# Handing x, conditioning and spatial matrices over transposed, fused dot products for conditioning, and a front on two column blocks of v

## The chip, the core and the metric

The program runs on one core of one Trainium2 chip. The metric is the device time of one execution in microseconds. The kernel before took 2926.15, 2928.23 and 2930.01 us in three runs (median 2928.23). What the host does to lay out the inputs before the launch is not part of the time. TensorE is written PE, VectorE DVE, ScalarE ACT, GpSimd POOL; SP is the engine on which nearly all transfers are issued.

## The reference, cut to what matters

```python
def gmlp_layer(x, c, ada_w, ada_b, norm_g, w_in, sgu_g, w_s, b_s, w_out):    # layer A
    shift, scale, gate = ada_mod(c, ada_w, ada_b, 3)      # split(silu(c) @ ada_w + ada_b)
    h = rms_norm(x, norm_g) * (1 + scale) + shift
    u, v, z = jnp.split(h @ w_in, 3, axis=-1)             # 1024 -> 3 x 2048
    u = jax.nn.gelu(u)
    v = rms_norm(jax.nn.gelu(v), sgu_g)
    w_causal = jnp.tril(w_s)                              # 8 groups of 128x128
    mixed = jnp.einsum('gts,bcsge->bctge', w_causal, v) + b_s...
    y = u * mixed * jax.nn.silu(z)
    return x + gate * (y @ w_out)
...
def shared_kv(...):        # its own shift, scale from kv_ada_w; h @ w_kv gives keys and values
def dilated_layer(...):    # layer B: its own shift, scale, gate; q and z from b_w_in,
                           # attention over three dilations, x + gate * (o * silu(z) @ w_out)
```

x is 2048 x 1024 float32. The conditioning vector c is one row of 1024; it goes through silu and three matrices (1024 x 3072, 1024 x 2048, 1024 x 3072) to give the shifts, scales and gates.

## The kernel before, in words

The 2048 tokens are worked in four quarters Q of 512. For each quarter layer A makes v (2048 columns), u, z and the output, and then layer B makes keys, values, q and its z; the attention of one quarter runs as side work beside layer A of the next. h stands transposed in SBUF: 1024 features as 8 tiles k of 128 rows, 512 tokens along a row. A float32 product is made of three rounded matmuls: h is split into a high part (hAh) and a low part (hAl), each weight tile into high and low too, and `mm3` issues high x high, low x high, high x low. The high part of a weight is a copy on ACT, the low part a subtraction on DVE (`split`).

For Q = 0 the dense product of v is written plainly: `dense` handles 512 columns j, loops over 2 pairs of token tiles, 8 tiles k and 2 token tiles. For Q = 1 to 3 v is made by `dense_s2` for two blocks of 1024 columns at a time, from 7 half-size products each: 14 products of 24 matmuls of 128x512. The operands of some of them are sums of quarters of h: s1, s2, s3 and s4. They come about so: `make_hA` makes h for the next quarter and stores it in DRAM (tile hd); `sums_A` loads it back as four pieces (m<-hd); DVE adds and subtracts them (s1, s3, s2, s4 in this order); each is split into high and low (sA). The order of the first six products of v is: block 4 with h's quarter 11, block 4 with 22, block 4 with 12, block 5 with 11, block 4 with s2, block 5 with 12. The gelu of the first product's columns is evacuated behind the third.

**Front.** `begin` serves Q = 0 and the first 512 columns of v. It loads x by token rows, squares on ACT, scales rows by 1/rms on DVE and transposes with PE into hf. Conditioning there: `add` accumulates 8 row tiles of the matrix times silu(c) into a 128x512 tile (DVE, scalar-tensor-tensor), one column group c of four at a time; `affine` sums that tile over its partitions by matmuls against a column of ones (pc_a). The product over these 512 columns is a plain float32 matmul (pd_v<-wf,hf, two hardware matmuls each), the other three blocks go through `dense`.

**Side work** stands in a list of generators; `tick` is called as PE's products go into the program and advances the generators by `rate` steps per unit; `drain` runs what is left. A z block is three `dense_s` blocks of 8 ticks' worth beside which `make_hA` of the next quarter advances at rate 0.9. Then comes `drain`, then v of the next quarter. The conditioning of shared keys and of layer B and the gate of layer A (`ada_acc`, `column_sums`, `ada_gate`) run as side work in Q = 0, the gate of layer B in Q = 3.

A scheduler with a cost model decides each engine's order when the program is built; the order is fixed from then on and each engine takes its queue strictly in it. Buffers come from pools: 6 large tiles (16 KB per partition), 8 weight tiles (w), 6 raw weight tiles (raw), 4 input tiles (xin), 6 evacuation tiles.

Of the kernel before, what the change touches and what calls it, by code (L numbers as in the profile page):

```python
# [15 lines left out]
ALU = mybir.AluOpType  # L16
# [18 lines left out]
def trunk(ctx, tc, out, x, c, a_ada_w, a_ada_b, a_norm_g, a_w_in, a_sgu_g, a_w_spatial,  # L35
          a_b_spatial, a_w_out, kv_ada_w, kv_ada_b, kv_norm_g, w_kv, k_norm_g, b_ada_w,
          b_ada_b, b_norm_g, b_w_in, b_q_norm_g, b_w_out, dbg=None):
# [27 lines left out]
    gd = dp.tile([2, D], F32, name="gd")  # L65
    wod = dp.tile([2, KT, P, 2, 512], F32, name="wod")
# [39 lines left out]
    ones = cp.tile([P, 1], F32, name="ones")  # L106
    nc.vector.memset(ones, 1.0)
# [3 lines left out]
    def columns(rows, nm):  # L111

        vec = evt(f"vec{nm}")
        nc.vector.memset(vec[:, 0:P], 0.0)
        off, o = [], 0
        for r in rows:
            n = r.shape[0] // P
            nc.sync.dma_start(vec[o:o + n, 0:P], r.rearrange("(k p) -> k p", p=P))
            off.append(o)
            o += n  # L120
        pv = pst(f"pv{nm}")
        nc.tensor.transpose(pv[:, 0:P], vec[:, 0:P], ident)
        t = cp.tile([P, o], F32, name=f"cols{nm}")
        nc.vector.tensor_copy(t, pv[:, 0:o])
        return [t[:, i:i + r.shape[0] // P] for i, r in zip(off, rows)]

    def load_x(t):
        xt = xp.tile([P, D], F32, tag="xin", name=f"x_{t}")
        nc.sync.dma_start(xt, x[t * P:(t + 1) * P, :])
        return xt  # L130

    xts = [load_x(0)]
    c_c, ang_c, aab_c = columns([c[0], a_norm_g[0], a_ada_b[0, 0:2 * D]], "a")
    sc = cp.tile([P, KT], F32, name="sc")
    xts += [load_x(1)]
    late = {}

    def late_constants():
        kg, bg, kb, bb, sgu, kn, qn = columns(
            [kv_norm_g, b_norm_g[0], kv_ada_b, b_ada_b[0, 0:2 * D], a_sgu_g[0], k_norm_g,  # L140
             b_q_norm_g[0]], "b")
        late.update(kg=kg, bg=bg, kb=kb, bb=bb, sgu=sgu)
        gqk = cp.tile([P, 1], F32, name="gqk")
        nc.vector.tensor_scalar(gqk, kn, qn, float(P) ** -0.5, ALU.mult, ALU.mult)
# [24 lines left out]
    def ada_acc(res, w, c0, nm):  # L169

        acc = evt(f"acc_{nm}")
        for k in range(KT):
            if k % 2 == 0:
                wt = xp.tile([P, 2, 512], F32, tag="xin", name=f"aw_{nm}{k}")
                nc.sync.dma_start(wt, w[k * P:(k + 2) * P, c0:c0 + 512].rearrange("(k p) n -> p k n", p=P))
            if k == 0:
                nc.vector.tensor_scalar(acc, wt[:, 0, :], sc[:, 0:1], None, ALU.mult)
            else:
                nc.vector.scalar_tensor_tensor(acc, wt[:, k % 2, :], sc[:, k:k + 1], acc, ALU.mult, ALU.add)
            if k % 2:  # L180
                yield
        res.append(acc)

    def column_sums(acc, nm):

        pc = pst(f"pc_{nm}")
        for j in range(4):
            nc.tensor.matmul(pc[:, j:j + 1], acc[:, j * P:(j + 1) * P], ones, start=True, stop=True)
        return pc[:, 0:4]

    later = []

    def delayed(gen):

        for _ in gen:
            for job in later:
                job[0] -= 1
            while later and later[0][0] <= 0:
                later.pop(0)[1]()
            yield  # L200
        while later:
            yield
            later.pop(0)[1]()
# [648 lines left out]
    def begin(aff):  # L852
# [31 lines left out]
        def transposes(c, prs=(0, 1)):  # L884
            if c not in pcs:
                pcs[c] = []
# [826 lines left out]
```

## Time and profile before

| what | value |
|---|---|
| three runs | 2926.15, 2928.23, 2930.01 us |
| profiled execution, span | 2930.7 us; the page gives no other time of it |
| granted TensorE clock, mean | 0.998 |
| first plain matmul of v | 18.53 us |
| first, second block of v done | about 53.3, 78.2 us |
| v of Q = 1, 2, 3 begins | 638.29, 1268.21, 1909.66 us |
| x loads from row layout | 16 of 512 KB, median 4.5 us from issue to landing |
| hd stores | 24 of 256 KB, median 5.0 us |
| loads of hd | 12 of 512 KB, median 6.4 us |

How to read the rows: in the timeline, a row is start, duration, engine, line of the kernel, operation, what it writes <- what it reads, form, count of neighbours put together, and in brackets the idle time of the engine before it with what ended it. In the table of groups, the fields behind the bar are total us, mean ns, and idle time before. SPq is SP's queue of transfers. Durations of neighbouring instructions overlap somewhat, so the pitch from start to start is the price in a stream.

### The profile page before, as it was taken

To read this page: it belongs to the slowest core of one execution; us is meant where nothing else is said; L and a number is where in the kernel's file an instruction comes from. 1 tells how busy PE (TensorE), PEld (TensorE's weight loads), DVE (VectorE), ACT (ScalarE), POOL (GpSimd) and SP (SyncE) were. 2 spreads that over 40 slices of the span, in tenths; PEclk is the share of its full clock that TensorE was granted. 3 is DMA by queue.
4 is the path that set the end of the run, shared out by engine and by line. 5 is a ranking of instruction groups with operands and counts; after the bars stand their busy time and mean duration, and the time that the engine had idled before them with its cause. 6 is when DMAs were issued, how large, how long until landed. Compare 5 with 4: busy or idle time off the path is not lost.

```text
span 2930.7 us, 45684 instructions
## 1 busy us (share of the span) xinstructions
PE 2890.4 (99%) x14642; PEld 2422.7 (83%) x14642; DVE 2166.7 (74%) x4038; ACT 1639.0 (56%) x3378; POOL 758.4 (26%) x1043
## 2 busy tenths in 40 slices
PE   8999999999999999999999999999999999999999
PEld 5788888888888878888888888888888888888887
DVE  6878666787777886877677776877769776888682
ACT  4323355767676365676555365674646366876441
POOL 1057522330000513501223213501414221122312
PEclk9999999999999999999999999999999999999999
DMA  8899976796889976887435976875337967789653
GB/s 285 272 311 336 308 244 184 257 306 203 282 294 315 334 241 210 265 289 249 158 120 202 344 226 203 296 262 162 105 109 260 322 202 224 256 271 332 216 172 112
DMA packets 393813, 713.54 MB, mean 243 GB/s; under 512 B 41723, under 2 KB 141277, under 8 KB 393573
## 3 DMA queue, kind: packets, MB, share of 16 engines
q1 hardware_dynamic: 393572, 710.63, 72.6%
q8 instruction: 116, 1.90, 0.3%
q14 instruction: 125, 1.02, 0.1%
HBM read 552.53 MB, written 157.95 MB: 242 GB/s over the span
## 4 chain that ended last, share of the span: by engine, by line
PE 40%; DMA 3%; issue 3%; DVE 3%; POOL 1%; ACT 1%; SPq 0%; POOLq 0%; ACTq 0%; DVEq 0%
PE po L1453 3%; PE pd_kv L280 3%; PE pd_z L324 2%; PE pd_z L322 2%; PE pd_z L323 2%; PE pd_o3a L280 1%; PE pd_u L322 1%; PE pd_u L324 1%; PE pd_u L323 1%; PE pd_o2a L280 1%; PE pd_v3b L280 1%; PE pf L1637 1%; PE pf L1638 1%; PE pf L1639 1%; DMA qt<-qd 1%
## 5 line engine op out<-in xcount | busy, mean ns | idle before, releaser
L280 PE MATMUL pd_kv<-w_kv,hkh 128*128 128x512 f32 x672 | 209.5, 393 | 1.4 <-DVE w_kv L252 1.3
L322 PE MATMUL pd_u<-hAh,w_u 128*128 128x512 f32 x512 | 207.5, 405 | 0.0
L322 PE MATMUL pd_z<-hAh,w_z 128*128 128x512 f32 x512 | 204.1, 399 | 0.0
L324 PE MATMUL pd_u<-hAh,w_u 128*128 128x512 f32 x512 | 201.0, 393 | 2.3 <-DVE w_u L252 2.3
L323 PE MATMUL pd_u<-hAl,w_u 128*128 128x512 f32 x512 | 200.2, 391 | 0.0
L324 PE MATMUL pd_z<-hAh,w_z 128*128 128x512 f32 x512 | 200.2, 391 | 0.0
L323 PE MATMUL pd_z<-hAl,w_z 128*128 128x512 f32 x512 | 199.5, 390 | 0.0
L1453 PEld LDWEIGHTS po<-kv,pT 128*128 128x128 f32 x1200 | 147.9, 192 | 13.0 <-ACT pT L1299 3.7
L251 ACT ACTIVATE w_u<-raw_u 128x512 fp32r<-128x512 f32 x128 | 79.2, 630 | 135.4 <-DMA raw_u<-in_a_w_in_dram 56.7
L1453 PE MATMUL po<-kv,pT 128*128 128x128 f32 x1200 | 151.2, 276 | 3.6 <-ACT pT L1299 2.5
L251 ACT ACTIVATE w_z<-raw_z 128x512 fp32r<-128x512 f32 x128 | 79.6, 628 | 133.9 <-PE pd_z L324 60.6
L280 PEld LDWEIGHTS pd_kv<-w_kv,hkh 128*128 128x128 f32 x672 | 125.9, 189 | 28.6 <-DVE w_kv L252 2.6
L1401 POOL TENSOR_TENSOR dg<-pr,ident 128x256 f32<-128x256 f32 x38 | 30.9, 813 | 437.2 <-DVE stat L1448 226.6
L252 DVE TENSOR_TENSOR w_z<-raw_z,w_z 128x512 fp32r<-128x512 f32 x128 | 109.4, 868 | 44.9 <-ACT w_z L251 44.6
L280 PE MATMUL pd_kv<-w_kv,hkl 128*128 128x512 f32 x336 | 131.2, 391 | 0.0
L1393 ACT ACTIVATE pr<-pr,stat,rt 128x256 f32<-128x256 f32 (+1 forms) x192 | 104.2, 544 | 33.2 <-DVE stat L1387 20.0
L1226 POOL TENSOR_SCALAR s_q<-s_q 128x4 f32<-128x4 f32 x96 | 26.6, 277 | 351.3 <-DVE s_q L1225 238.8
L252 DVE TENSOR_TENSOR w_u<-raw_u,w_u 128x512 fp32r<-128x512 f32 x128 | 94.1, 745 | 30.8 <-ACT w_u L251 30.0
L324 PEld LDWEIGHTS pd_u<-hAh,w_u 128*128 128x128 f32 x512 | 96.4, 188 | 24.2 <-DVE w_u L252 3.1
L251 ACT ACTIVATE w_q<-raw_q 128x512 fp32r<-128x512 f32 x144 | 88.8, 627 | 48.3 <-PE pd_kv L280 11.2
L252 DVE TENSOR_TENSOR w_q<-raw_q,w_q 128x512 fp32r<-128x512 f32 x144 | 95.8, 687 | 24.9 <-ACT w_q L251 22.9
L324 PEld LDWEIGHTS pd_z<-hAh,w_z 128*128 128x128 f32 x512 | 96.1, 188 | 20.7
(904 smaller groups left out, 8553.1 us busy)
## 6 DMA issues: line engine op xcount, KB each, us to landing
raw_q<-in_b_w_in_dram SPq DMA_DIRECT2D x144, 256.0 KB, 3.4
w_o<-wtd SPq DMA_DIRECT2D x72, 512.0 KB, 5.2
raw_u<-in_a_w_in_dram SPq DMA_DIRECT2D x128, 256.0 KB, 4.2
raw_z<-in_a_w_in_dram SPq DMA_DIRECT2D x128, 256.0 KB, 3.6
wtd<-cs SPq DMA_DIRECT2D x56, 512.0 KB, 4.1
qt<-qd SPq DMA_DIRECT2D x96, 260.0 KB, 3.6
raw_v<-in_a_w_in_dram SPq DMA_DIRECT2D x96, 256.0 KB, 4.1
od<-ot SPq DMA_DIRECT2D x96, 256.0 KB, 3.0
```

What stands on the lines that cost most here:

```text
L251: nc.scalar.activation(hi, src, AF.Copy)
L252: nc.vector.tensor_tensor(lo, src, hi.bitcast(F32), ALU.subtract)
L280: last_mm[0] = nc.tensor.matmul(pt, a, u[:, w, :], start=f, stop=e, skip_group_check=more)
L322: nc.tensor.matmul(pts[i], wh, hh[:, k, :], start=k == 0, stop=False)
L323: nc.tensor.matmul(pts[i], wh, hl[:, k, :], start=False, stop=False)
L324: nc.tensor.matmul(pts[i], wl, hh[:, k, :], start=False, stop=k == KT - 1)
L1393: nc.scalar.activation(pr[:, i, :], pr[:, i, :], AF.Exp, bias=mneg[:, i:i + 1], scale=u["rt"][:, h:h + 1], accum_out=lsum[:, i:i + 1])
L1401: nc.gpsimd.tensor_tensor(dg, prev, ident.unsqueeze(1).broadcast_to([P, hp, P]), ALU.mult)
L1453: nc.tensor.matmul(po[:, h * P:(h + 1) * P], u["pT"][h // hp][:, h % hp, j, :], u["kv"][:, j, kh, 1, :], start=j == 0, stop=j == nk - 1)
L1637: nc.tensor.matmul(pt, yb[:, 0, k, :], w_[:, 0, :], start=k == 0, stop=False)
L1638: nc.tensor.matmul(pt, yb[:, 0, k, :], w_[:, 1, :], start=False, stop=False)
L1639: nc.tensor.matmul(pt, yb[:, 1, k, :], w_[:, 0, :], start=False, stop=k == KT - 1)
```

## The change

The host now hands over, laid out differently: x as before and also transposed (xt: quarter, feature, k, token); the three conditioning matrices transposed and cut into tiles of 128 outputs x 1024 (a_ada, kv_ada, b_ada); the spatial matrices transposed (spatial); the vectors of norms and biases packed as columns of one 128 x 106 array (cols). The computation is the same.

- Conditioning: 128 outputs stand on the partitions and their 1024 weights along the row; `ada_dot` multiplies by silu(c), broadcast to all partitions (scb), sums along the row and adds the bias, in one DVE instruction and a second that reads the accumulator. The sums over partitions on PE are gone. The gate of layer B moves from Q = 3 to Q = 0. Gates go to DRAM (gd) as columns.
- `make_hA` loads x by rows for the squares and xt for the values; 1/rms goes through DRAM (rd) to be broadcast as a row (rb). Values are multiplied by rb (DVE), then scale and shift (ACT), high part (ACT), store to hd, low part (POOL), k by k for all 512 tokens. There are no PE transposes. It yields 27 times where it yielded 20, at the same rate.
- `begin` sums squares with PE against ones, makes the broadcast of 1/rms with PE, and then for k = 0 to 7 does both column blocks 0 and 1 by three rounded matmuls, with the conditioning of k + 1 made beside. `dense` then makes blocks 2 and 3.
- The spatial matrices are one load.

```diff
+    def ada_dot(dst, w, b):
+        nc.vector.tensor_tensor_reduce(out=w, in0=w, in1=scb, scale=1.0, scalar=b, op0=ALU.mult,
+                                       op1=ALU.add, accum_out=dst)
+    def ada_col(dst, w, j0, bo, nm):
+        for j in range(KT):
+            t = xp.tile([P, D], F32, tag="xin", name=f"aw_{nm}{j}")
+            nc.sync.dma_start(t, w[j0 + j])
+            ada_dot(dst[:, j:j + 1], t, bo[:, j:j + 1])
+            yield
...
+    def ada_gate(w, bo, i, nm):
+        col = sp.tile([P, 16], F32, tag="rt", name=f"gc_{nm}")
+        yield from ada_col(col, w, 2 * KT, bo, nm)
+        nc.sync.dma_start(gd[i:i + 1, :].rearrange("o (k p) -> p (o k)", p=P), col[:, 0:KT])
...
     def make_hA(res, Q, aff):
...
+        zs = [xp.tile([P, 2, QT], F32, tag="xin", name=f"xT{Q}_{k2}") for k2 in range(0, KT, 2)]
+        for i, z in enumerate(zs):
+            nc.sync.dma_start(z, xt[Q, :, 2 * i:2 * i + 2, :])
+        yield
+        nc.sync.dma_start(rd[Q].rearrange("t p -> p t"), r[:, 0:TPQ])
         yield
         yield
-        for t in range(TPQ):
-            nc.scalar.activation(xts[t], xts[t], AF.Copy, scale=r[:, t:t + 1])
-            yield
-        for pr in range(2):
-            for k2 in range(0, KT, 2):
-                norm_T(xts[2 * pr:2 * pr + 2], pr, [hA + aff], f"a{Q}_{pr}_", (k2,))
-                yield
+        rb = bcast(rd[Q:Q + 1].rearrange("o t p -> o (t p)"), f"rb{Q}")
+        yield
+        yield
+        for k in range(KT):
+            z = zs[k // 2][:, k % 2, :]
+            nc.vector.tensor_tensor(z, z, rb, ALU.mult)
+            yield
+            h = evt(f"h_a{Q}_{k}")
+            nc.scalar.activation(h, z, AF.Identity, scale=aff[0][:, k:k + 1], bias=aff[1][:, k:k + 1])
+            nc.scalar.activation(hA[0][:, k, :], h, AF.Copy)
+            nc.sync.dma_start(hd[:, :, k, :].rearrange("r p t -> p r t"),
+                              h.rearrange("p (r t) -> p r t", r=2))
+            nc.gpsimd.tensor_tensor(hA[1][:, k, :], h, hA[0][:, k, :].bitcast(F32), ALU.subtract)
+            yield
...
     def begin(aff):
...
+        for k in range(KT):
+            h = xT[:, k, :]
+            if k == 1:
+                nc.vector.tensor_tensor(h, h, rb, ALU.mult)
+            if k:
+                nc.scalar.activation(h, h, AF.Identity, scale=aff[0][:, k:k + 1], bias=aff[1][:, k:k + 1])
+                split(hA[0][:, k, :], hA[1][:, k, :], h)
+            if k + 1 < KT:
+                units(k + 1)
+                affine(k + 1)
+            if k + 2 < KT:
+                load(k + 2)
+                nc.gpsimd.tensor_tensor(xT[:, k + 2, :], xT[:, k + 2, :], rb, ALU.mult)
+            for j in range(2):
+                for t in range(TPQ):
+                    sl = slice(t * P, (t + 1) * P)
+                    mm3(pts[j][t], hA[0][:, k, sl], hA[1][:, k, sl], us[k][j], k == 0, k == KT - 1)
```

**Where the order moves: DVE in the front.** aw is a piece of the conditioning matrix, acc_a its accumulation, affa scale and shift, pc_a the sums from PE, colsa the vectors, r_a 1/rms. Before, from the first accumulation on:

```order
L878 TENSOR_SCALAR acc_a_273<-aw_207,sc 128x512
L879 SCALAR_TENSOR_TENSOR acc_a_273<-aw_207,sc,acc_a_273 128x512 x7
L902 TENSOR_TENSOR affa_194<-pc_a_318,colsa 128x2
L903 TENSOR_TENSOR affa_193<-pc_a_318,colsa 128x2
L904 SCALAR_TENSOR_TENSOR affa_193<-affa_193,colsa 128x2
L878 TENSOR_SCALAR acc_a_343<-aw_222,sc 128x512
L941 TENSOR_SCALAR x_216<-x_216,r_a_315 128x1024
L879 SCALAR_TENSOR_TENSOR acc_a_343<-aw_222,sc,acc_a_343 128x512
```

Now, from the third dot product (k = 1) on, the rows up to the weights of k = 2; L152 ISA is the dot and, with one column, the reading of its accumulator, L188 the low parts of weights w_v and of h (hAl):

```order
L152 ISA aw_315,affa_181<-aw_315,scb,vecs 128x1024
L152 ISA affa_181 128x1
L188 TENSOR_TENSOR w_v_1_0_365<-raw_v_1_0_366,w_v_1_0_365 128x512
L188 TENSOR_TENSOR w_v_1_0_370<-raw_v_1_0_371,w_v_1_0_370 128x512
L829 SCALAR_TENSOR_TENSOR affa_180<-affa_180,vecs 128x1
L152 ISA aw_378,affa_180<-aw_378,scb,vecs 128x1024
L152 ISA affa_180 128x1
L829 SCALAR_TENSOR_TENSOR affa_180<-affa_180,vecs 128x1
L152 ISA aw_378,affa_181<-aw_378,scb,vecs 128x1024
L152 ISA affa_181 128x1
L188 TENSOR_TENSOR hAl_187<-xT_188,hAh_186 128x512
L188 TENSOR_TENSOR w_v_2_0_410<-raw_v_2_0_411,w_v_2_0_410 128x512
```

The chain of eight accumulations and the wait for PE's sums are gone; two dots for each k stand among the subtractions.

**SP at the boundary, ahead of v of Q = 1.** hd is h in DRAM, m1 the loads of its four pieces, raw_v the weights of v (raw_v1511 those of the fourth product), zd the stores of z. Before:

```order
L259 DMA raw_v14t4_0_6037<-wt4_3_125 128x512
L708 DMA hd_104<-h_a1_1_6_0_5892 128x512
L259 DMA raw_v14t4_1_6042<-wt4_3_125 128x512
L1240 DMA zd_101<-zb00_2_5914 128x512
L1240 DMA zd_101<-zb00_3_5917 128x512
L828 DMA m1_1_5976<-hd_104 128x1024
L259 DMA raw_v14t4_2_6047<-wt4_3_125 128x512
L259 DMA raw_v14t4_3_6052<-wt4_3_125 128x512
L259 DMA raw_v1421_0_6091<-in_a_w_in_dram 128x512
```

Now:

```order
L1099 DMA zd_101<-zb10_0_5844 128x512
L1099 DMA zd_101<-zb10_1_5847 128x512
L723 DMA hd_105<-h_a1_5_5851 128x2x256
L723 DMA hd_105<-h_a1_6_5857 128x2x256
L723 DMA hd_105<-h_a1_7_5863 128x2x256
L195 DMA raw_v1511_0_6039<-in_a_w_in_dram 128x512
L195 DMA raw_v1511_1_6044<-in_a_w_in_dram 128x512
L195 DMA raw_v1511_2_6049<-in_a_w_in_dram 128x512
L743 DMA m1_1_5872<-hd_105 128x1024 x2
L195 DMA raw_v1511_3_6054<-in_a_w_in_dram 128x512
```

Before, the last store to hd stood ahead of the z stores of two product groups; now three stores stand behind the last z stores, and two of the four loads from hd stand behind them, with weights of the fourth product between and the last of these (raw_v1511_3) behind.

**ACT at the boundary of Q = 2.** zb are copies of z, h_a2 the shifted h of tile k, hAh2 its high part, st_v2u the copy of the first product, m2_0 the gelu, jk2 the squares, sA20 and sA21 the high parts of the sums, w_v2511 the weights of the fourth product. Before, from the last z copy on:

```order
L1239 ACTIVATE zb11_1_12316<-st_z1bu1_11953 128x512
L251 ACTIVATE w_v24t4_2_12393<-raw_v24t4_2_12394 128x512
L251 ACTIVATE w_v24t4_3_12398<-raw_v24t4_3_12399 128x512
L251 ACTIVATE sA20_12324<-m2_1_12323 128x1024
L251 ACTIVATE w_v2421_0_12437<-raw_v2421_0_12438 128x512
L630 ACTIVATE st_v2u00_12379<-pd_v2a0_12331 128x512
L251 ACTIVATE sA20_12324<-m2_1_12323 128x1024
L630 ACTIVATE st_v2u01_12380<-pd_v2a1_12332 128x512
L251 ACTIVATE w_v2421_1_12442<-raw_v2421_1_12443 128x512
L251 ACTIVATE w_v2421_2_12447<-raw_v2421_2_12448 128x512
L251 ACTIVATE w_v2421_3_12452<-raw_v2421_3_12453 128x512
```

Now, from the last z copies on, and a little later:

```order
L1098 ACTIVATE zb11_0_12159<-st_z1bu0_11834 128x512
L187 ACTIVATE w_v24t4_3_12261<-raw_v24t4_3_12262 128x512
L1098 ACTIVATE zb11_1_12162<-st_z1bu1_11835 128x512
L721 ACTIVATE h_a2_5_12165<-xT2_4_11327,affa1_181,affa0_180 128x512
L721 ACTIVATE h_a2_6_12171<-xT2_6_11328,affa1_181,affa0_180 128x512
L722 ACTIVATE hAh2_10962<-h_a2_5_12165 128x512
L722 ACTIVATE hAh2_10962<-h_a2_6_12171 128x512
L721 ACTIVATE h_a2_7_12177<-xT2_6_11328,affa1_181,affa0_180 128x512
L566 ACTIVATE st_v2u00_12242<-pd_v2a0_12194 128x512
L722 ACTIVATE hAh2_10962<-h_a2_7_12177 128x512
```

```order
L187 ACTIVATE w_v2511_2_12362<-raw_v2511_2_12363 128x512
L187 ACTIVATE sA20_12187<-m2_1_12186 128x1024 x2
L758 ACT_TABLE_LOAD
L758 ACTIVATE m2_0_12189<-pd_v2a0_12194 128x512
L758 ACTIVATE m2_0_12189<-pd_v2a1_12195 128x512
L760 ACTIVATE jk2_0_0_12345,sqv2_0_12182<-m2_0_12189 128x512
L760 ACTIVATE jk2_0_1_12348,sqv2_1_12183<-m2_0_12189 128x512
L187 ACTIVATE w_v2511_3_12367<-raw_v2511_3_12368 128x512
L187 ACTIVATE sA21_12188<-m2_1_12186 128x1024
```

h of tiles 5 to 7, which before was done ahead of the z copies, now follows them; the splits of the sums moved from ahead of the fourth product's weights to a place just before their last tile, with a table load and the gelu and squares of the first product between.

391 lines of the change are left out of this document (124 added, 267 removed).

## The prediction

> **What bounds the kernel now.** I read the page's busy shares first, then the table by windows for the start, then the timeline of single engines at the places that the change touches.
>
> ```profile
> span 2930.7 us, 45684 instructions
> PE 2890.4 (99%) x14642; PEld 2422.7 (83%) x14642; DVE 2166.7 (74%) x4038; ACT 1639.0 (56%) x3378; POOL 758.4 (26%) x1043
> ```
>
> TensorE is busy for 2890 of 2931 us, so nearly every matmul taken out of its queue shortens the run, and a wait on TensorE lengthens it. The profiled execution (2930.7) is 2.5 us above the median of the three times, 2928.23; I make the sum on the span and subtract 2.5 at the end.
>
> ```profile
> 0.00:18.50 18.50, 8.28 (x51) 7.15 (x51) 8.00 (x17) 5.42 (x10) 5.13 (x41) 1.00 0.92 301
> 18.50:53.30 34.80, 34.19 (x112) 16.88 (x112) 27.36 (x49) 16.94 (x33) 1.44 (x2) 1.00 1.00 341
> ```
>
> Columns: window, its length, busy time of PE, PEld, DVE, ACT, POOL, clock, DMA share, GB/s. The first 18.5 us wait for data and conditioning; then TensorE is full.
>
> ```profile
> 18.53 3.70 PE L929 MATMUL pd_v<-wf,hf 128*128 128x512 f32 x8 [0.25 <-ACT hf L913]
> 53.31 0.73 PE L280 MATMUL pd_v<-w_v,hAh 128*128 128x512 f32 x2
> 78.17 0.62 PE L280 MATMUL pd_v<-w_v,hAh 128*128 128x512 f32 x2
> ```
>
> So the first column block of v takes 18.53 to 53.31 in plain float32, the second, in three rounded products each, until 78.17. The pitch of one 128x512 matmul is 0.227 us (24 of them in 5.44, rows below), a triple 0.68.
>
> **The front.** Now both blocks run side by side: for each of 8 row tiles k of the weights, 2 blocks x 4 token tiles x 0.68 = 5.44 us. When can they start? Ahead of the first product come 2.1 MB of transposed x, 0.05 of vectors, 1.05 of conditioning (at 301 GB/s they are in by 10.7 us) and 0.5 of weights (12.3). Then DVE makes two dot products, ACT the rounded h, DVE the low parts. VectorE's prices:
>
> ```profile
> L879 DVE SCALAR_TENSOR_TENSOR acc_a<-aw,sc,acc_a 128x512 f32<-128x512 f32 x28 | 21.0, 751 | 0.9
> L833 DVE TENSOR_TENSOR m<-m 128x1024 f32<-128x1024 f32 x3 | 3.7, 1221 | 0.1
> 49.48 3.10 DVE L252 TENSOR_TENSOR w_v<-raw_v,w_v 128x512 fp32r<-128x512 f32 x5
> 94.92 0.15 DVE L213 TENSOR_TENSOR affk<-pc_ksh,colsb 128x4 f32<-128x4 f32 x1
> ```
>
> The fused 128x1024 dot is not in this trace. Below stands a 128x1024 tensor-tensor, 1.22 us, above two 128x512 scalar-tensor-tensors, 1.50; I take 1.35, being nearest to the first, and 0.15 for the row that reads its accumulator (as the other 128x4 operation). Per k VectorE then has two dots 2 x 1.50, one small 0.15 and three subtractions at pitch 0.61: 5.0 us (4.7 to 5.3), under TensorE's 5.44; DMA has 1.57 MB, 4.6 us at 341 GB/s, under it too. So TensorE bounds from k = 1. First product near 15.5; k = 1 near 22 (its conditioning lands at 4.8 MB, 15.9; two dots, h, low parts, 6 us); then 7 x 5.44 = 38.1, and 1 for slack: the third block begins near 61 instead of 78.2, **-17** (between 59 and 64: -19 to -14).
>
> ```profile
> 51.37 1.28 ACT L843 ACT_TABLE_LOAD   x1
> 57.04 1.68 ACT L251 ACTIVATE w_v<-raw_v 128x512 fp32r<-128x512 f32 x3
> ```
>
> Against it: eight tiles are evacuated at once. Before, a table load and four took 51.37 to 57.04, so 1.1 each; eight take 10.1. On ACT two of the third block's weight tiles stand behind them; TensorE reaches the first of these after 6 x 1.36 = 8.2 us, and it is split at about 11.3. **+2** (0 to 3).
>
> **TensorE work that goes away after 78 us.**
>
> ```profile
> 92.96 0.94 PE L188 MATMUL pc_ksh<-ones,acc_ksh 128*128 128x1 f32 x8
> 93.76 0.72 PE L280 MATMUL pd_v<-w_v,hAh 128*128 128x512 f32 x2
> 82.35 1.02 PE L232 MATMUL pg_ga<-acc_ga,ones 128*1 128x512 f32 x2
> 83.30 0.73 PE L280 MATMUL pd_v<-w_v,hAh 128*128 128x512 f32 x2
> 603.21 2.89 PE L280 MATMUL pd_z0ba<-w_z0bt,hob 128*128 128x512 f32 x12
> 605.94 0.60 PE L695 MATMUL pt_a<-ident,x 128*128 128x128 f32 x4
> 609.14 2.88 PE L280 MATMUL pd_z0bb<-w_z0b,hob 128*128 128x512 f32 x12
> 632.85 5.60 PE L280 MATMUL pd_z0bb<-w_z0b,hob 128*128 128x512 f32 x24
> ```
>
> Column sums: 8 groups, each 92.96 to 93.76 = 0.80: -6.4. Gate sums: 0.95 each, three of four behind 78 us: -2.9. Transposes of Q = 1 to 3: 24 groups; a product with one takes 603.21 to 609.14 = 5.93, one without 632.85 to 638.29 = 5.44; 24 x 0.49 = -11.8. Together **-21**. VectorE's part of this (96 accumulations become 48 dots) is off the path: it is 74% busy, and both forms cost alike (96 x 0.75 against 48 x 1.50, 72 each).
>
> **The boundaries between quarters.** This is where the change adds a wait. The generator that makes the normalized h of the next quarter now has 27 steps instead of 20 and gets 0.9 x 24 = 21.6 of them during the z block. The rest is put out after it: h of tiles 5, 6, 7 stands on ACT behind the last two z copies, their three stores to hd behind these on SP, and behind the stores the loads that the sums s1 to s4 need.
>
> ```profile
> 638.29 0.62 PE L280 MATMUL pd_v1a<-w_v,hAh 128*128 128x512 f32 x2
> 640.79 1.23 ACT L1239 ACTIVATE zb<-st_z0bu 128x512 f32<-128x512 f32 x2 [1.41 <-DVE st_z0bu L575]
> 635.11 0.33 SPq L708 DMA_DIRECT2D hd<-h_a  x1
> 642.74 1.23 DVE L832 TENSOR_TENSOR m<-m 128x1024 f32<-128x1024 f32 x1 [1.43 <-DMA m<-hd]
> 1268.21 0.62 PE L280 MATMUL pd_v2a<-w_v,hAh 128*128 128x512 f32 x2
> 1272.37 0.61 ACT L1239 ACTIVATE zb<-st_z1bu 128x512 f32<-128x512 f32 x1
> 1261.17 0.32 SPq L708 DMA_DIRECT2D hd<-h_a  x1
> 1269.15 1.22 DVE L832 TENSOR_TENSOR m<-m 128x1024 f32<-128x1024 f32 x1
> 1909.66 0.61 PE L280 MATMUL pd_v3a<-w_v,hAh 128*128 128x512 f32 x2
> 1901.58 0.33 SPq L708 DMA_DIRECT2D hd<-h_a  x1
> 1911.47 1.23 DVE L832 TENSOR_TENSOR m<-m 128x1024 f32<-128x1024 f32 x1
> ```
>
> Call z the start of v (the first, fifth and ninth row). Before, the last store went out at z-3.2, -7.0, -8.1, and the first sum began 7.6, 8.0, 9.9 us later, in good time. Now the last z copy ends at z+3.7 to +4.8, and five ACT instructions at pitch 0.53 put the last store at z+6.4 to +7.5. Plus 7.6 to 9.9: sums from z+14 to z+17.4. Who waits? The sums stand on DVE ahead of weights. s2 is there 3.5 us on (three at pitch 1.14). Then, for Q = 2 and 3, ACT has two splits of sums, a table load, two gelus and two squares before the last weight tile of the fourth product:
>
> ```profile
> 659.24 1.28 ACT L843 ACT_TABLE_LOAD   x1
> 660.53 1.08 ACT L843 ACTIVATE m<-pd_v1a 128x512 f32<-128x512 f32 x2
> 661.50 0.63 ACT L845 ACTIVATE jk<-m 128x512 f32<-128x512 f32 x1
> 662.73 1.05 ACT L251 ACTIVATE sA<-m 128x1024 fp32r<-128x1024 f32 x1
> 663.68 0.62 ACT L251 ACTIVATE w_v14t<-raw_v14t 128x512 fp32r<-128x512 f32 x1
> ```
>
> 659.24 to 662.73 is 3.5 us; with 2 x 0.95 for the splits, 0.6 for the tile and 0.7 for its low part it is ready 3.5 + 1.9 + 3.5 + 1.3 = 10.2 after the sums begin, z+24.2 to +27.6. TensorE wants it at 3 x 5.44 + 3 x 1.36 = z+20.4. For Q = 1 it is the fifth product's first tile, some 12 after the sums, wanted at z+21.8. Either way TensorE stands 4 to 7 us. It may also stand up to 1 earlier for h of tile 5, which comes off the same wait. I take 5 each, the low end because DVE and ACT, idle by then, may catch up: **+15** (0 to +22).
>
> ```profile
> 135.00:140.00 5.00, 3.12 (x16) 2.42 (x14) 4.76 (x8) 0.51 (x1) 0.20 (x1) 0.93 0.36 99
> 140.00:145.00 5.00, 5.00 (x19) 4.42 (x19) 4.44 (x9) 1.60 (x3) 0.00 (x0) 0.50 1.00 307
> ```
>
> Such a stall can cost the clock too: after 1.9 idle us of five, the granted clock was 0.50 for the next five, a loss of 2.5. I add 1 per boundary, **+3** (0 to +7.5).
> [...]
>
> Sum: -17 + 2 - 21 + 15 + 3 = **-18**: 2930.7 - 18 - 2.5 = **2910 us**.
>
> **Rivals.**
> *The boundary is covered after all.* If the stores issue as ACT frees early and land in the 7.6 of the first boundary, TensorE would wait at most 1 to 2 us. For it: before had six to eight us to spare. Against: the order puts them behind z's copies. -36 and +3: 2895. Chance 0.20.
> *The fused dot is slow.* At half rate, 2.44 us, VectorE has 7.2 per k, not 5.0; the front is then VectorE's, 7 x (7.2 - 5.44) = 12 later: 2922. Against: a two-source operation with a scalar at 128x512 takes 751 ns where five plain ones take 3.10 us, so nothing halves there. Chance 0.10. [...]
> *Slower: the path through DRAM.* The stores now have two pieces of 1 KB per partition where they had one of 2, three come within 2 us, and two 512 KB loads wait for all. It decides once a boundary costs 12 us (36 / 3). Were the way from store to sum 19 us (twice 9.9), the tile would be ready at z+7+19+10.2 = 36, a stall of 16 and the clock 2.5: 55 in all, +19: 2945. For it: SP is one queue, and weights of the fourth and fifth product stand behind the loads. Against: 7.6 to 9.9 three times. Chance 0.12.
> *The change doesn't do what it says in the front*: TensorE waits for conditioning at every k, so that the blocks end near 72 and not 61: 2921. Chance 0.08.
>
> **How the numbers follow.** Forecast 0.50, rivals 0.20, 0.10, 0.12, 0.08. The forecast's own range is 2898 to 2922 (both ends of the boundary); with the rivals to two tenths left out, 2889 to 2928. Within 0.2% (5.9 us, about what can be told from no change) falls a part of the slow dot, of the late front and of the long boundary: 0.11; slower 0.11; faster 0.78.
>
> **What would show it.** The third block's first matmul between 59 and 64 us; no L695 transposes; dots of 1.2 to 1.5 us in VectorE's rows; waits of 4 to 7 us on TensorE at the three starts of v plus 20, released by weights or sums, and the windows behind them below clock 1. Wrong would be a dot over 1.7, no such waits, or waits over 10.

## The result: slower, 2979.5 us

The changed kernel took 2979.52 us (median of four runs, 2976.24 to 2983.25) beside 2927.19 us of the kernel before on the same chip (2921.05 to 2930.01): a ratio of 1.0184, 95% interval 1.0172 to 1.0196. Forecast were 2910 us, with 2928 as the upper end. The sign was wrong and the error is about 70 us, so something much larger than any term of the sum was missed.

### The profile after

The head of the page, to be read against the two lines of the kernel before:

```profile
span 2981.5 us, 45378 instructions
PE 2889.6 (97%) x14519; PEld 2434.3 (82%) x14519; DVE 2140.4 (72%) x3997; ACT 1659.8 (56%) x3403; POOL 772.2 (26%) x1042
```

TensorE has 123 matmuls fewer than before, but is as busy as before (2889.6 us against 2890.4), and its share fell from 99% to 97%. The work that went away was given back in two ways: TensorE waits, and behind the waits its matmuls run at half clock (0.50 granted from 577 to 581 us and from 680 to 685, rows below). The view of TensorE's waits names what it waited for (total us, times, longest):

```profile
PE pd_q00b L216 <- DVE st_q01u L511: 8.9, 1, 8.9
PE pd_q20b L216 <- DVE st_q21u L511: 7.9, 1, 7.9
PE pd_q10b L216 <- DVE st_q11u L511: 7.4, 1, 7.4
PE pt_b L637 <- DVE xr L984: 6.8, 2, 6.4
PE pd_v1a L216 <- ACT w_v14t L187: 4.3, 1, 4.3
PE pd_v2b L216 <- ACT w_v L187: 3.3, 1, 3.3
PE pd_v3b L216 <- ACT w_v L187: 3.1, 1, 3.1
```

The last three are the boundary waits of the prediction. The first three were not in it: they lie at the products of q (pd_q00, pd_q10, pd_q20), ahead of each z block, where the change leaves the products as they were and only takes out some transposes of x. To see which waits matter for the end I took the first matmul of each stage in both traces:

| stage begins | before, us | after, us | shift |
|---|---|---|---|
| third block of v, Q = 0 | 78.2 | about 84.3 | +6.1 |
| u, Q = 0 | 126.5 | 128.0 | +1.5 |
| z, Q = 0 | 237.8 | 233.5 | -4.3 |
| keys and values, Q = 0 | 414.0 | 417.8 | +3.8 |
| product q00a, Q = 0 | 558.2 | 565.9 | +7.7 |
| z block beside Q = 1 (z0ba) | 603.2 | 620.0 | +16.8 |
| v of Q = 1 | 638.3 | 652.7 | +14.4 |
| its first product of a sum | 661.2 | 680.6 | +19.4 |
| product q10a, Q = 1 | 1188.2 | 1209.0 | +20.8 |
| z1ba | 1233.1 | 1264.0 | +30.9 |
| v of Q = 2 | 1268.2 | 1296.6 | +28.4 |
| first product of a sum, Q = 2 | 1290.0 | 1328.2 | +38.2 |
| product q20a, Q = 2 | 1829.6 | 1869.0 | +39.4 |
| z2ba | 1874.9 | 1922.9 | +48.0 |
| v of Q = 3 | 1909.7 | 1955.6 | +45.9 |
| first product of a sum, Q = 3 | 1933.3 | 1986.9 | +53.6 |
| end | 2930.7 | 2981.5 | +50.8 |

The 84.3 is worked out: the second tile k of the front starts at 46.17 (row below), and seven tiles at 5.44 lie between it and the third block. In the lower half the loss comes in two kinds of steps: 9.1, 10.1 and 8.6 us from a product of q to the z block, and 5.0, 9.8 and 7.7 from the start of v to its first product of a sum.

### Place one: the products of q

SP's queue, then ACT and TensorE at the first of the three places:

```profile
565.35 0.37 SPq L710 DMA_DIRECT2D rd<-r_a  x1
565.81 0.93 SPq L195 DMA_DIRECT2D raw_q00t<-wt  x2
...
575.59 0.32 SPq L175 DMA_DIRECT2D rb<-rd  x1
```

```profile
578.33 0.63 ACT L187 ACTIVATE w_q00t<-raw_q00t 128x512 fp32r<-128x512 f32 x1 [13.21 <-DMA raw_q00t<-wt]
```

```profile
580.43 7.11 PE L216 MATMUL pd_q00b<-w_q00t,hob 128*128 128x512 f32 x24 [8.91 <-DVE st_q01u L511]
```

TensorE's wait is put down to a DVE copy, but that copy stands behind a weight subtraction, that behind ACT's copy of the weight, and ACT sat idle for 13.21 us for a load. The 24 matmuls behind the wait took 7.11 us where the 24 before it took 5.60: 1.5 us more, at a granted clock of 0.50 from 577 to 581. What the DMA engines did meanwhile stands in the table by windows (last three figures: clock, DMA share, GB/s):

```profile
565.00:569.00 4.00, 4.00 (x19) 3.32 (x18) 2.01 (x4) 0.13 (x1) 3.51 (x8) 1.00 0.06 1
569.00:577.00 8.00, 2.52 (x12) 1.75 (x10) 0.00 (x0) 0.00 (x0) 1.21 (x3) 0.97 0.72 33
577.00:581.00 4.00, 0.57 (x2) 0.51 (x3) 2.00 (x4) 1.88 (x4) 0.00 (x0) 0.50 0.87 215
```

For 12 us from the issue of rd on, little is moved. Two explanations fit this one trace. The load rb waits for rd in SP's queue, and every weight behind it waits with it (the queue's gap from 567 to 575.6). Or the store rd itself, 2 KB that go out as 512 pieces of four bytes, holds up the two weights issued half a microsecond behind it (565.81, landed at 578). I took the first to be true, and a run showed that it was the second.

### Place two: the front

TensorE, SP, then DVE and POOL in the first 47 us:

```profile
6.12 1.87 PE L809 MATMUL pssq<-one,sqT 128*128 128x1 f32 x8
...
22.82 1.71 PE L809 MATMUL pssq<-one,sqT 128*128 128x1 f32 x8
...
33.00 0.73 PE L216 MATMUL pd_v<-w_v,hAh 128*128 128x512 f32 x2 [1.28 <-ACT hAh L844]
36.58 1.10 PE L216 MATMUL pd_v<-w_v,hAh 128*128 128x512 f32 x3 [2.85 <-DVE w_v L846]
...
46.17 2.11 PE L216 MATMUL pd_v<-w_v,hAh 128*128 128x512 f32 x8 [0.59 <-ACT hAh L187]
```

```profile
8.40 9.17 SPq L838 DMA_DIRECT2D raw_v<-in_a_w_in_dram  x2
```

```profile
36.45 1.77 DVE L847 TENSOR_TENSOR hAl<-xT,hAh 128x512 fp32r<-128x512 f32 x1
...
39.82 2.29 DVE L152 CUSTOM_DVE_ANT_0 aw<-aw,scb,vecs 128x1024 f32<-128x1024 f32 x1
```

```profile
31.29 9.75 POOL L865 TENSOR_TENSOR xT<-xT,rb 128x512 f32<-128x512 f32 x6 [4.43 <-ACT rb L850]
```

Three things are to be seen. TensorE sums the squares in eight groups of eight matmuls, 1.7 us each, with filler between, and is through with them at 24.5 only, though the last square stood at 12.6; the first product of v follows at 33.00, not at 15.5. A weight tile waits 9 us on SP, since by the program some of the squares sit in the raw buffers until TensorE has read them. And while POOL multiplies six tiles, DVE's operations take up to two and a half times their price (1.77 us for a low part that takes 0.69 from 47 us on), and the second tile k begins at 46.17 and not at 22: 17.5 us of that were lost ahead of the first product, the rest behind it. The rest of the front then runs at 5.44 a tile as forecast.

### Place three: the boundary, as forecast

SP, DVE and TensorE behind the start of v of Q = 1 at 652.7:

```profile
658.66 2.81 SPq L723 DMA_DIRECT2D hd<-h_a  x3
...
664.40 0.80 SPq L743 DMA_DIRECT2D m<-hd  x2
```

```profile
669.21 1.23 DVE L747 TENSOR_TENSOR m<-m 128x1024 f32<-128x1024 f32 x1 [1.00 <-DMA m<-hd]
```

```profile
680.62 1.22 PE L216 MATMUL pd_v1a<-w_v14t,sA 128*128 128x512 f32 x2 [4.32 <-ACT w_v14t L187]
```

```profile
680.00:685.00 5.00, 4.38 (x13) 3.65 (x14) 4.52 (x7) 5.00 (x10) 0.00 (x0) 0.50 0.31 82
```

With z the start of v, the stores go out at z+6.0 to z+8.8 (forecast: the last at z+6.4 to 7.5, so a little late), the sums begin at z+16.6 (forecast: z+14 to 17.4), TensorE waits 4.3 us, released by a weight tile of the fifth product, and runs at half clock behind it (0.50 from 680 to 685).

### The profile page after: what moved, and what is told of

Its sections match the earlier page's. It is cut to its first block, busy times and chain, and to the rows that moved or that the text cites. A ratio compares the mean times of both kernels' runs of the same rounds, so it can differ in the third digit from the quotient of the medians.

```text
span 2981.5 us, 45378 instructions
## 1 busy us (share of the span) xinstructions
PE 2889.6 (97%) x14519; PEld 2434.3 (82%) x14519; DVE 2140.4 (72%) x3997; ACT 1659.8 (56%) x3403; POOL 772.2 (26%) x1042
## 4 chain that ended last, share of the span: by engine, by line
PE 63%; DMA 5%; DVE 3%; issue 3%; ACT 2%; POOL 1%; SPq 0%; POOLq 0%; DVEq 0%; ACTq 0%
PE pd_kv L216 6%; PE po L1314 4%; PE pd_z L260 3%; PE pd_z L258 3%; PE pd_z L259 3%; PE pd_u L260 3%; PE pd_u L258 3%; PE pd_u L259 3%; PE pd_o3a L216 1%; PE pd_o1a L216 1%; PE pd_o2a L216 1%; PE pm L900 1%; PE pd_v3b L216 1%; PE pq L1204 1%; PE pf L1498 1%
## 5 line engine op out<-in xcount | busy, mean ns | idle before, releaser
L188 DVE TENSOR_TENSOR w_z<-raw_z,w_z 128x512 fp32r<-128x512 f32 x128 | 102.2, 806 | 53.5 <-ACT w_z L187 53.1
L188 DVE TENSOR_TENSOR w_q<-raw_q,w_q 128x512 fp32r<-128x512 f32 x144 | 96.7, 694 | 24.4 <-ACT w_q L187 23.4
L260 PEld LDWEIGHTS pd_z<-hAh,w_z 128*128 128x128 f32 x512 | 96.1, 188 | 20.8
L259 PEld LDWEIGHTS pd_z<-hAl,w_z 128*128 128x128 f32 x512 | 96.3, 188 | 18.1
```

Source lines behind the costliest of these rows:

```text
L188: nc.vector.tensor_tensor(lo, src, hi.bitcast(F32), ALU.subtract)
L259: nc.tensor.matmul(pts[i], wh, hl[:, k, :], start=False, stop=False)
L260: nc.tensor.matmul(pts[i], wl, hh[:, k, :], start=False, stop=k == KT - 1)
```

## The experiments

Each kernel computes all of the reference. The kernel before ran beside them each time, at medians of 2924 to 2926 us.

| run | us, median | ratio to before, 95% interval |
|---|---|---|
| change as it is | 2979.5 | 1.0184 (1.0172 to 1.0196) |
| 1/rms broadcast by TensorE | 2946.7 | 1.0079 (1.0059 to 1.0099) |
| the same, rd still stored, nobody reads it | 2975.9 | 1.0173 (1.0159 to 1.0187) |
| the same store as 16-byte pieces | 2951.6 | 1.0088 (1.0070 to 1.0106) |
| the same store issued by ACT | 2955.9 | 1.0106 (1.0088 to 1.0124) |
| side work ahead of the boundary at rate 1.2 | 2963.0 | 1.0133 (1.0108 to 1.0159) |
| sums of squares in the front on DVE | 2970.5 | 1.0154 (1.0139 to 1.0169) |
| the front's multiplications on DVE | 2971.8 | 1.0160 (1.0140 to 1.0179) |
| side work of Q = 0 at rate 2.5 | 2993.3 | 1.0238 (1.0223 to 1.0254) |
| four mends together | 2917.6 | 0.9974 (0.9962 to 0.9985) |
| the four without the boundary's | 2932.0 | 1.0024 (1.0013 to 1.0035) |
| four mends and rate 2.5 | 2925.6 | 1.0000 (0.9989 to 1.0011) |

### 1/rms without the detour through DRAM

```diff
-        nc.sync.dma_start(rd[Q].rearrange("t p -> p t"), r[:, 0:TPQ])
...
+        for t in range(TPQ):
+            sl = slice(t * P, (t + 1) * P)
+            nc.scalar.activation(diag[:, sl], ident, AF.Copy, scale=r[:, t:t + 1])
...
+            nc.tensor.matmul(prb[:, sl], one, diag[:, sl], start=True, stop=True)
...
-        rb = bcast(rd[Q:Q + 1].rearrange("o t p -> o (t p)"), f"rb{Q}")
...
+        nc.scalar.activation(rb, prb, AF.Copy)
```

> The changed kernel with one edit: in the generator for the next quarter, 1/rms is broadcast to all partitions by four 128x128 matmuls of ones against a diagonal, and no longer stored to DRAM (rd) and loaded back (rb). The loads of transposed x stay. Theory A (SP's queue): the load rb stands in SP's queue four rows behind the store rd, waits for its landing (9.7 us at the first quarter boundary), and the weights of q behind it come late. Then the waits of 8.9, 7.4 and 7.9 us on pd_q00b, pd_q10b and pd_q20b and the half clock behind each go: 2979.5 - 27 = 2953 us (2947 to 2959). Rival (burst): the 2 MB of transposed x that are loaded just ahead fill the DMA engines, and the weights are late for that; then the three waits stay and the time is 2974 to 2982.

2946.7 us: 33 us gone, with the three waits at q. In its trace the way from the product of q to the z block takes 44.4 us each time, against 54.1, 55.0 and 54.0 in the changed kernel. The detour is the largest single loss. The transposed loads of x were left as they were, so it isn't these. What the run doesn't tell is which half of the detour it is, the store or the load that waits for it.

### The store alone

```diff
+        nc.sync.dma_start(rd[Q].rearrange("t p -> p t"), r[:, 0:TPQ])
```

(put back into the kernel of the run above; nothing reads rd)

> The broadcast of 1/rms is made by TensorE as in the run without the detour, but its store to DRAM (512 pieces of four bytes) is still issued; nobody reads it back. Theory (the loss is the wait of the load rb in SP's queue, which keeps the weights behind it from being issued): as without the detour, about 2947 us, and no wait of 7 to 9 us at the three first products of q. Rival (the small pieces of the store themselves hold up the weights on the DMA engines): the waits stay, about 2975 us.

2975.9 us: my theory fell, and the rival holds. Without any load that waits for rd, the loss is back, and in the same place (from q to the z block 54.7, 54.0 and 54.3 us). SP issues the weights right behind the store, and they land 12 us later:

```profile
565.15 0.37 SPq L710 DMA_DIRECT2D rd<-r_a  x1
565.62 0.93 SPq L195 DMA_DIRECT2D raw_q00t<-wt  x2
```

```profile
577.85 0.63 ACT L187 ACTIVATE w_q00t<-raw_q00t 128x512 fp32r<-128x512 f32 x1 [12.90 <-DMA raw_q00t<-wt]
```

The store is worth 29 us of the 33 (2975.9 - 2946.7). What the load and its wait add, 3.6, is inside the two intervals.

### How many pieces, and from which queue

Both runs start from the kernel of the run above, in which nothing reads rd. The first changes the layout of rd:

```diff
-        nc.sync.dma_start(rd[Q].rearrange("t p -> p t"), r[:, 0:TPQ])
+        nc.sync.dma_start(rd[Q].rearrange("t p -> (t p)").rearrange("(p t) -> p t", t=TPQ), r[:, 0:TPQ])
```

> As the run with the store that nobody reads, but the same 2 KB go out as 128 pieces of 16 bytes, not 512 of four. Theory (what costs is the number of pieces, during which the transfers behind it hardly move): a stop of about 3 us and not 11.6, which the weights' lead covers; no wait of 7 us at the three first products of q, 2947 to 2953 us. Rival (any store of these narrow columns costs a fixed time): waits of 7 us as with 512 pieces, about 2976 us.

2951.6 us, and no wait at q. The tile view of rd gives the time from issue to landing; first in the run above, with four-byte pieces, then here, with 16-byte ones:

```profile
DMA to landing us min/median/max: 9.4/9.7/9.9
```

```profile
DMA to landing us min/median/max: 1.4/1.9/2.5
```

So the same 2 KB land five times sooner as 128 pieces. The order of SP's queue and its wait for the store's input are the same in both runs, so it is the pieces that cost; their number and their size changed together, and which of the two counts these runs do not tell. The transfers still stop for 2.4 us and then move at 196 GB/s, which the weights' lead covers (from q to the z block 44.8, 45.3 and 44.5 us). The 4.9 us above the run without the store fit a longer wait for x1 near 410 us (9.8 us, there 5.4), ahead of the first store:

```profile
570.60:573.00 2.40, 2.40 (x13) 1.97 (x12) 1.72 (x3) 0.00 (x0) 2.23 (x4) 1.00 0.03 1
573.00:575.00 2.00, 2.00 (x11) 1.65 (x10) 0.00 (x0) 0.00 (x0) 1.68 (x5) 1.00 0.65 196
```

The second run issues the 512 pieces from ACT:

```diff
-        nc.sync.dma_start(rd[Q].rearrange("t p -> p t"), r[:, 0:TPQ])
+        nc.scalar.dma_start(rd[Q].rearrange("t p -> p t"), r[:, 0:TPQ])
```

> As the run with the store that nobody reads, 512 pieces of four bytes, but issued by ScalarE and not from SP's queue. Theory A (the store holds up what stands behind it in SP's queue): the weights pass it, no waits, about 2947 us. Theory B (while the 512 pieces are made and sent the transfers of all queues stand): waits of about 7 us as before, about 2976 us.

2955.9 us, nearer to theory A's time. The first two places are free of waits over 0.4 us (45.1 and 45.8 us from q to the z block); at the third there are waits up to 2.0, and the way takes 49.6. And the transfers do not simply pass the store either. It is issued at 565.95, and behind it:

```profile
565.00:567.00 2.00, 2.00 (x10) 1.68 (x9) 0.00 (x0) 0.53 (x1) 1.09 (x2) 1.00 0.92 331
567.00:571.00 4.00, 4.00 (x19) 3.30 (x19) 3.28 (x6) 3.23 (x7) 2.18 (x5) 1.00 0.19 38
571.00:575.00 4.00, 4.00 (x19) 3.23 (x18) 3.40 (x6) 2.90 (x7) 3.46 (x7) 1.00 0.53 146
```

For 4 us the core's transfers fall to 38 GB/s from another queue too, as theory B has it; they recover sooner (146 GB/s from 571 to 575, where the store from SP left 33 until 577). The two weights that were late went out at 562.25 here and at 565.62 from SP, since SP had first stood for the store's input; those 3.4 us put them ahead of the stop. How much of the 20 us (2975.9 - 2955.9) is this earlier issue and how much the separate queue, these runs leave open.

### The boundary

```diff
-                rate[0] = 0.9
+                rate[0] = 1.2
```

> The changed kernel with the rate of the generator for the next quarter 1.2 in place of 0.9, so that its 27 steps end before the z block does. Theory B (late store): the stall of 4.3, 3.3 and 3.1 us at the start of v with what precedes it in h of tiles 5 to 7 and the half clock behind it comes from the three stores that are put out after the z block; then these go and each of the three places gives back 5 to 7: 2979.5 - 18 = 2961 us (2956 to 2967). Rival: the stall is in ACT's queue (table load, gelu, squares ahead of the weights) whenever the sums come, or the denser steps only move it into the z block: 2974 to 2982.

2963.0 us, 16.5 less. The waits at the starts of v shrink to under 2 us; but with the generator ahead of itself the store rd comes earlier too, and its waits move to other products of q (the largest below; 3.0 to 3.4 us at the later quarters):

```profile
PE pd_q01b L216 <- DVE st_q01v L511: 6.9, 1, 6.9
...
PE pd_v3a L216 <- DVE w_v L188: 1.9, 1, 1.9
```

The price without that disturbance comes from the four mends with and without this one:

> The four mends without the one of the boundary (side work ahead of it at rate 0.9 again; broadcast by TensorE, sums of squares and multiplications on VectorE). Theory (late hd costs 16 to 22 us over three boundaries on its own): 2917.6 + 16.5 to 22.5 = 2934 to 2940 us, with waits of 3 to 4.5 us at the starts of v of the second, third and fourth quarter plus 20. Rival (with the other waits gone the boundary is covered): as the run with four, 2918 to 2922 us.

2932.0 us against 2917.6: 14.4 us, a little under the 16 to 22 of theory; the waits stand where they should, and the rival (covered) is out. Between the two traces the way from the z block to the first product of a sum differs by 4.6, 4.0 and 2.1 us, 10.8 in all, so the boundary's own price is 11 to 14 us:

```profile
PE pd_v1a L216 <- ACT w_v14t L187: 4.2, 1, 4.2
...
PE pd_v2b L216 <- ACT w_v L187: 3.0, 1, 3.0
PE pd_v3b L216 <- ACT w_v L187: 3.0, 1, 3.0
```

### The front

```diff
-            for t in range(TPQ):
-                nc.tensor.matmul(pqs[t][:, 0:1], sqs[k][:, t * P:(t + 1) * P], one[:, 0:1],
-                                 start=k == 0, stop=k == KT - 1)
+            if k:
+                nc.vector.tensor_tensor(sqs[0], sqs[0], sqs[k], ALU.add)
...
+        for t in range(TPQ):
+            nc.tensor.matmul(pqs[t][:, 0:1], sqs[0][:, t * P:(t + 1) * P], one[:, 0:1], start=True, stop=True)
```

> The changed kernel with the sum of squares of the front added up over k on DVE (idle until 23 us) and only four column matmuls behind it, in place of 32, with more keep-warm transposes between. Theory C1 (chain on PE): the squares are done at 12.6 us, but 32 matmuls of one column at 1.7 us for each four, with transposes between, end at 25.4; then the first matmul of v comes at 21 to 24 in place of 33.0: 2979.5 - 10 = 2969 us (2965 to 2973). Rival: conditioning data or DVE sets the start, and the first matmul moves by 3 at most: 2975 to 2981.

2970.5 us, 9 less: theory's size, but not all of it in theory's place. The first product of v starts at 26.47 instead of 33.00 (expected 21 to 24), the second tile k at 38.0 instead of 46.2; POOL still slows DVE there: four low parts take 6.81 us.

```profile
30.54 6.81 DVE L188 TENSOR_TENSOR w_v<-raw_v,w_v 128x512 fp32r<-128x512 f32 x4
```

The third block of v then begins at 77.4, 7.0 us earlier than in the changed kernel (84.4). But in the fourth block a new wait of 4.13 us for a weight, behind which one matmul takes 0.73 us where single rows of the same trace have 0.39, takes most of this back, and u begins only 1.1 us earlier (126.9 against 128.0). Where the rest of the 9 us of the whole run comes from was not followed.

```profile
103.65 0.73 PE L216 MATMUL pd_v<-w_v,hAh 128*128 128x512 f32 x1 [4.13 <-DVE w_v L188]
```

The other half moves the six multiplications from POOL to DVE:

```diff
-                nc.gpsimd.tensor_tensor(xT[:, k + 2, :], xT[:, k + 2, :], rb, ALU.mult)
...
-            if k == 1:
+            if k:
                 nc.vector.tensor_tensor(h, h, rb, ALU.mult)
```

> The changed kernel with the six multiplications of transposed x by 1/rms in the front moved from POOL (31.3 to 41 us) to DVE, one ahead of each k. Theory C2 (DVE and POOL slow each other): DVE's 128x512 operations between 31.7 and 39.9, which take 1.75 us each, go back to 0.69, the dot there from 2.29 to 1.28; the second k begins at 39 to 41 in place of 46.2, with 1 us given back as DVE has 0.6 more per k: 2979.5 - 6 = 2973.5 us (2970 to 2977). Rival: these operations are slow for their operands or the DMA traffic; they stay at 1.7 and the time is 2978 to 2984.

2971.8 us, 8 less, although DVE has six operations more; the second tile k begins at 39.7, the third block at 77.9 and u 4.0 us earlier. The same two instructions that took 1.77 and 2.29 us:

```profile
33.14 0.69 DVE L847 TENSOR_TENSOR hAl<-xT,hAh 128x512 fp32r<-128x512 f32 x1
...
34.35 1.28 DVE L152 CUSTOM_DVE_ANT_0 aw<-aw,scb,vecs 128x1024 f32<-128x1024 f32 x1
```

This shows that POOL slowed them, and that the fused dot's own price is 1.28. A tensor-scalar among them, which reads one tensor (L843), went from 1.49 to 0.54. If each of the two-input operations stood still for a whole multiplication of POOL (9.75 / 6 = 1.63), 0.69 would become 2.3; measured was 1.77, at 1.68 from start to start, near POOL's own pitch; how the two share their time the rows do not tell.

### The side work of the first quarter

One more unforeseen wait, 6.4 us at 409, is for x1, the input of layer B. DVE scales x1 in place and waits until the store of x1 (issued at 402.82) has landed, amid transfers at 392 GB/s; it does not wait for a load, as the expectation below has it:

```profile
409.07 1.09 PE L637 MATMUL pt_b<-ident,xr 128*128 128x128 f32 x4 [6.44 <-DVE xr L984]
```

```profile
408.17 0.75 DVE L984 TENSOR_SCALAR xr<-xr,r_b 128x1024 f32<-128x1024 f32 x1 [2.25 <-DMA x1d<-xr]
```

```profile
405.00:410.00 5.00, 0.93 (x5) 0.96 (x6) 2.52 (x4) 1.23 (x3) 1.43 (x3) 0.59 1.01 392
```

I put this down to side work that starts later: the gate's first operation on DVE stands at 82.1 us, before at 64.4. Running it faster should mend that:

```diff
-    rate[0] = 2.2
+    rate[0] = 2.5
```

> The changed kernel with the side work of the first quarter at rate 2.5 instead of 2.2. Theory (the third block of v begins 6 us late and the side work with it, so that the load of x1 for the first kv product comes late): the wait of 6.4 us on pt_b at about 410 us goes, and with it up to 2 us at half clock: 2971 to 2974 us. Rival (the wait comes from the longer list of side work's transfers, not from its start): the wait moves or stays, 2978 to 2983 us.

2993.3 us: 14 slower. This theory fell as a remedy. The wait on x1 is gone, but others took its place, at the output product of layer A and at q:

```profile
PE pd_q02b L216 <- DVE st_q02u L511: 5.8, 1, 5.8
PE pd_o L216 <- ACT w_o L187: 4.9, 1, 4.9
```

The rival (the wait moves) is nearer, but it had 2978 to 2983. These two waits alone are longer than the one removed (10.7 us against 6.4), and there are others, of 2.0 us at z and 2.5 at v; why the faster side work makes them was not followed. With the four mends, whose side work starts earlier, the wait on x1 is 2.3 us without any change of rate.

### All together

> The changed kernel with four mends: 1/rms broadcast by TensorE, rate 1.2 of the side work ahead of each boundary, sums of squares in the front added on VectorE, and the front's multiplications by 1/rms on VectorE. Theory (four separate causes): the single gains 33, 16.5, 9 and 8 add up, 2979.5 - 66.5 = 2913 us, which is faster than the kernel before by 0.3 to 0.5%. Rival (the causes overlap, so that a wait mended in one place comes back in the next): 2925 us or more, the same as before.

2917.6 us, 0.15 to 0.38% faster than the kernel before. The single gains add up to 66 (33 + 16.5 + 9 + 7.7), together they are 62 (2979.5 - 2917.6): by the times, four separate causes that hardly overlap. No wait is left at the three places of q; TensorE's are these and smaller ones:

```profile
PE pd_v L216 <- DVE w_v L188: 4.7, 2, 4.0
...
PE prb L834 <- ACT diag L833: 2.8, 1, 2.8
```

> The same four mends and the side work of the first quarter at rate 2.5. Theory: 6 to 8 us below the run with four, near 2906 us. Rival: as the run with four, since with an earlier third block the wait on pt_b has gone already.

2925.6 us, 8 slower than with the four: neither theory nor rival; the same moved waits as at rate 2.5 alone (6.4 us at pd_q02b, 4.4 at pd_o). This version is the kernel before in time; the one with four mends beats both.

## Why the prediction was wrong

The sum by its own terms, against the shifts of the trace:

| term | predicted | in the trace | what the runs say |
|---|---|---|---|
| third block of v (front, late weights) | -17 + 2 | +6.1 | -9.7 with both mends of the front |
| TensorE work removed | -21 | -20.2 | no run of its own |
| boundary and clock | +15 + 3 | +22.5 | 11 to 16.5 |
| rd and rb | 0 | +27.8 | 33 |
| side work of Q = 0 | 0 | +8.1 and +3.9 | not settled |
| rest | 0 | +2.6 | not followed |
| sum (before 2.5 is taken off) | -18 | +50.8 | |

**The step that failed most is one that isn't in the working: 1/rms through DRAM was priced at nothing.** The description of the change names the store and the load; the part on the cost counted matmuls, dots, evacuations and hd's stores, and passed over a transfer of 2 KB. Of the transfers in the generator of the next quarter it priced those of hd alone. The medians quoted ahead of it (4.5 to 6.4 us) would not have given the price either, being those of 256 and 512 KB; but a store that scatters single four-byte elements was to be seen in the code, and in the order of SP's queue it stands among the weights of q. A bound from both sides was called for there and not made.

**The front: the sum started from the wrong chain.** "Then DVE makes two dot products, ACT the rounded h" sets the first product at 15.5 by transfers and conditioning. The sum of squares was missing: 64 matmuls in eight groups, 2.2 to 2.7 us from group to group with the filler, then 1/rms, its broadcast, the multiplication. It ended at 33.0. The second half is "k = 1 near 22": it took DVE's prices from rows in which POOL was idle, beside a step that put six multiplications on POOL. From the second tile on the term held: 5.44 a tile, and dots of 1.28 plus 0.08, where 1.35 plus 0.15 were taken. With both mends the third block begins at 68.5, 9.7 ahead of the kernel before; the 17 is not reached, since the chain through the squares still puts the first product at 24.7. Behind it a wait of 4.0 us for a weight, at 95.7, and slower matmuls (up to 0.80 us in v, where the median is 0.39) take part of that back, and u begins at 120.1, 6.4 ahead.

**TensorE's work removed was right in kind and near in size**, but that the trace gives -20.2 is partly luck. It is -4.6 from the third block to u, -5.8 from there to z, -2.4, -2.5 and -2.1 in the three z blocks, -2.8 at the end. Of the 24 groups of transposes only 14 lay in the z blocks; the other ten, 4.9 us at the prediction's 0.49, lay between the products of q and the z block, where the loss through rd hides them (27.8 + 4.9 = 32.7, near the 33 of the run without the detour). And the 5.8 is not all removed work: the four column sums there are 3.2 at the prediction's 0.80, and the kernel before ran at half clock near 140 us (0.50 from 140 to 145 in the prediction's windows), where the changed kernel had 1.00.

**The boundary was right in place and mechanism**, waits of 3.1 to 4.3 us released by ACT's weight tiles where 4 to 7 were forecast, and ahead of them, as it feared, waits for late tiles of h (0.9, 2.7 and 1.9 us). In the table of shifts it is 5.0, 9.8 and 7.7 us, half clock included, above the 18 forecast; taken alone, 11 to 16.5. The clock: a wait of 4.3 us was followed by five us at 0.50, one of 2.85 in the front (1.28 idle and 0.73 busy ahead of it) by windows at 0.72 and 0.59. That is more than the 1 us per boundary I added.

**The rivals.** The slow dot is out: 1.28 us at 128x1024 with POOL idle, hardly more than the 1.22 of a plain tensor-tensor, where half rate would have been 2.44. The 2.29 us rows are POOL's doing. The covered boundary is out by the waits. The path from the last hd store to the sums took 7.7 us (661.47 to 669.21), not 19, so the slower rival, which had the sign, had the wrong place. The late front ("the blocks end near 72") had the right direction; they ended near 84, for reasons other than waits of each tile on its conditioning.

Two of its sums do not come out of their terms, without bearing on what failed: with boundary and clock at nothing the forecast's low end is 2892 and not 2898, and the slower rival gives 2947 and not 2945.

## What to carry to other kernels

Don't price a transfer by its bytes alone, and price it for what stands behind it: the same 2 KB landed after 9.7 us in 512 pieces and after 1.9 in 128 (medians of the two runs in which nobody reads them), and in 512 pieces they kept the weights behind them from landing for about 12 us, three times; the engine named in the wait (DVE) was three steps away from the cause. When a change frees the bounding engine in one place, list every chain that leads to its first instruction there, the sums and reciprocals too; and take an engine's prices from rows in which its neighbour is as busy as it will be (a low part took 0.69 us on DVE beside an idle POOL and 1.77 beside its multiplications). Two explanations that fit one trace are told apart by keeping one half of the step: the store that nobody read settled in one run what reading the queue had got wrong.

## What was not expected of the hardware

- A store of 512 four-byte pieces landed after 5.5 to 9.7 us in the changed kernel, 9.4 to 9.9 in the run in which nobody reads it, 7.2 to 9.1 from ACT. The core's transfers stand for about 4 us around it (1 GB/s from 565 to 569; SP had issued nothing from 560.8 to 565.3) and then crawl at 33 GB/s for 8 more when it comes from SP; from ACT the low stretch is 4 us at 38 GB/s and 4 more at 146. With 128 pieces of 16 bytes the stop is 2.4 us. The pieces themselves are soon out: in the changed kernel's trace all 512 packets start between 566 and 567. From 567 to 569 none starts. The 140 packets that start from there to 577 take 0.66 us on the mean (71.7% of 16 engines' 8 us), the 1317 of the next 8 us 0.09 (95.6%). What holds the 140 up the trace does not show.
- POOL's elementwise multiplications slow DVE's operations beside them: a low part from 0.69 to 1.77 us, the dot from 1.28 to 2.29, a tensor-scalar from 0.54 to 1.49. POOL's six took 1.63 each, where another group of the same shape in the changed kernel took 1.30 (total us, then mean ns behind the bar); whether DVE slowed them no run shows:

```profile
L1506 POOL TENSOR_TENSOR of<-of,xr 128x512 f32<-128x512 f32 x32 | 41.5, 1297 | 136.1 <-DVE of L1505 106.4 <-DVE stat L1251 22.2 <-DVE stat L1274 7.4
```

- In the front of the changed kernel a group of eight 128x1 float32 matmuls took 1.7 us of TensorE (1.71 from 22.82), 0.21 each, about as much as a rounded 128x512 matmul each (0.227 in the prediction). One column of plain float32 cost as much there as 512 rounded ones; the column sums of the kernel before, also eight 128x1 matmuls, took 0.94 (row at 92.96 in the prediction), 0.12 each. What makes the difference is not shown.
